# Hybrid S5 / short-conv layer on one core: context tiles normed by ScalarE, first channel block moved forward in the head

## The chip, the cores and the metric

One core of a Trainium2 chip. The metric is the device time of one execution in microseconds (us); less is better. Engines: PE is TensorE, DVE is VectorE, ACT is ScalarE, POOL is GpSimd, SP is SyncE. SP and POOL start DMA transfers, each through a queue of its own (q1 is SP's and ACT's, q0 is POOL's); all transfers share 16 DMA engines.

## What is computed

One layer of a diffusion backbone, cut to what matters here (512 latent tokens, 256 context tokens, 2048 channels):

```python
shift, scale, gate = split(silu(c) @ w_ada + b_ada)      # adaLN, once for c, once for c_ctx
h  = layernorm(x)   * (1 + scale)   + shift              # latent, 512 x 2048
hc = layernorm(ctx) * (1 + scale_c) + shift_c            # context, 256 x 2048
u, z_s5, v, bg, cg, z_cv = split(h @ w_in)
u_c = hc @ w_in[:, :1024]
... state-space scan over u_c then u, GLU, short convolution, output product, gate, layernorm
```

The change is in the layernorms, the adaLN sums and the first products with w_in.

## The kernel before

The kernel writes its instructions in one fixed order; engines run their own instructions in that order and wait for each other by semaphores. The function `head` does everything up to `u` and `u_c`. All products with w_in are in split float32: a weight tile `raw` (128x512, from `w_u`) becomes `whi` (ACT) and `wlo` (DVE, the remainder), a channel block of the input becomes `hi` and `lo`, and three matmuls are added up.

**Token tiles.** Six tiles of 128 tokens x 2048 channels: 0 to 3 latent (x), 4 and 5 context (ctx); x4 and x5 below are the two context tiles. For tile q, `stats(q)` runs four BN_STATS and a BN_AGGR on DVE and a Sqrt on ACT; `norm(q)` makes the reciprocal deviation in five short DVE operations (`rstd_b`) and applies it to the tile in place, one DVE pass over 128x2048 (`wa<-wa,mv,sd`); `turn(q)` transposes the tile on PE in 16 pieces (`acc<-ident,wa`, four to a PSUM bank), and ACT copies each out into the channel-major `xl[k]` (latent) or `xc[k]` (context). DVE takes half of tile 5's copies.

**adaLN.** For each of 16 channel blocks k, `ada(k, 0)` and `ada(k, 1)` multiply one weight tile each (`w_ada`, 1 MB) into `aps`, eight matmuls each. `combine(k)` has two steps: ACT copies `aps` out (`part`); PE transposes it and DVE reduces it into `ss` (shift and scale). `mod(k)` then writes `hi` (ACT) and, in place and `lo`, two DVE operations for each of latent and context. `lat(k)` is nine matmuls of 128x512, `cxt(k, hf)` twelve of 128x256, for each half.

**Buffers and queues.** Token tiles and adaLN tiles share seven 1 MB buffers, `wa` (`RB = 7`). `fill()` gives a new tile the buffer whose last reader stands first in the program. SP's queue takes, in this order: the four latent tiles, w_ada tiles (0,0) and (0,1), x4, three `raw`, x5, then the other `raw` (five buffers of 256 KB). POOL's queue takes all other w_ada tiles, (1,0) and (1,1) first, each as soon as its buffer is free. x5 takes the buffer of tile 0, so SP starts it once tile 0 has been transposed.

**Order.** Tiles 0, 1, 2 are turned, then come `ada(0)`, tile 3, `ada(1)`, `lat(0)`, tile 4, tile 5, `ada(2)`, `cxt(0, 0)`, `mod(1)`, `cxt(0, 1)`, `ada(3)`, `mod(2)`; from there a loop runs one channel block after the other up to k = 15. Behind the head stand some 800 us of products, scan and output, in the same order before and after the change but for the short operations below. A list of planned times (`_Clock`) places background work there.

Of the kernel before, what the change touches and what calls it, by code (L numbers as in the profile page):

```python
# [8 lines left out]
F32 = mybir.dt.float32  # L9
F32R = mybir.dt.float32r  # L10
I32 = mybir.dt.int32
AF = mybir.ActivationFunctionType
OP = mybir.AluOpType

P = 128
# [129 lines left out]
def tile_hybrid_s5_shortconv(  # L145
# [8 lines left out]
    ve, ac = _Timed(nc.vector, "dve", clk), _Timed(nc.scalar, "act", clk)  # L154
# [8 lines left out]
    prm = rest.__enter__()  # L163
# [13 lines left out]
    def slot(name, dt=F32):  # L177
        return base.tile([P, SEQ], dt, name=name, tag="hk", bufs=32)

    def cslot(name, dt=F32):  # L180
        return hcp.tile([P, CTX], dt, name=name, tag="hc", bufs=16)
# [13 lines left out]
    def tt(out, a, b, op, e=None):  # L195
        (e or ve).tensor_tensor(out, a, b, op=op)
# [3 lines left out]
    raws, his = {}, {}  # L200
    items = []

    def pair():
        return [base.tile([P, 512], F32R, name=nm, tag=nm, bufs=3) for nm in ("whi", "wlo")]
# [6 lines left out]
    def load():  # L211
        j = st["load"]
        r = base.tile([P, 512], F32, name="raw", tag="raw", bufs=5)
        sp.dma_start(r, items[j][0])
        raws[j] = r
        st["load"] += 1
# [262 lines left out]
    def head():  # L479
        with pool(name="head", bufs=1) as hp, \  # L480
# [14 lines left out]
            rows, used, near = {}, set(), []  # L495

            def fill(e=None):
                while len(rows) < len(ring):
                    n = len(rows)
                    if n >= RB and ring[n - RB] not in used:  # L500
                        return
                    t = rows[ring[n]] = hp.tile([P, D], F32, name="wa", tag="wa", bufs=RB)
                    a, b = ring[n]
                    if a != "x":
                        (e or gp).dma_start(t, wada_ss[a, b])
                    elif b == 0:
                        for f in range(4):
                            sp.dma_start(t[:, f * 512:(f + 1) * 512], x_in[0:P, f * 512:(f + 1) * 512])
                    else:
                        sp.dma_start(t, x_in[b * P:(b + 1) * P] if b < 4 else ctx_in[(b - 4) * P:(b - 3) * P])  # L510
# [13 lines left out]
            aps, cps = aps[:, 0:256], aps[:, 256:512]  # L524
            for k in range(KT):
                xl[k], xc[k] = slot("xl") if k < KT - 1 else hp.tile([P, SEQ], F32, name="xl15"), cslot("xc")
            sts, rss = {}, {}

            def stats(q):
                stt = hp.tile([P, 4, 6], F32, name="bst", tag="bst", bufs=2)  # L530
                mv = hp.tile([P, 2], F32, name="mv", tag="mv", bufs=2)
                for f in range(4):
                    ve.bn_stats(stt[:, f], rows["x", q][:, f * 512:(f + 1) * 512])
                    yield
                ve.bn_aggr(mv, stt)
                sts[q] = mv
                rss[q] = rstd_a(prm, mv[:, 1:2])
                yield

            def norm(q):  # L540
                yield from rstd_b(rss[q], sts[q][:, 1:2])
                t = rows["x", q]
                ve.tensor_scalar(t, t, sts[q][:, 0:1], rss[q][:, 3:4], op0=OP.subtract, op1=OP.mult)

            def run(*gs):
                gs = list(gs)
                while gs:
                    for g in list(gs):
                        try:
                            next(g)  # L550
                        except StopIteration:
                            gs.remove(g)

            def turn(q):
                t = rows["x", q]
                for k4 in range(4):
                    b = acc[(4 * q + k4) % 7 if q < 4 else 3 + k4]
                    for k in range(4):
                        kk = k4 * 4 + k
                        pe.transpose(b[:, k * P:(k + 1) * P], t[:, kk * P:(kk + 1) * P], ident)  # L560
                    for k in range(4):
                        kk = k4 * 4 + k
                        dst = xl[kk][:, q * P:(q + 1) * P] if q < 4 else xc[kk][:, (q - 4) * P:(q - 3) * P]
                        if q == 5 and k4 > 1:
                            ve.tensor_copy(dst, b[:, k * P:(k + 1) * P])
                        else:
                            ac.activation(dst, b[:, k * P:(k + 1) * P], AF.Copy)
                    if q == 5 and k4 == 0:
                        mod_c(0)
                used.add(("x", q))  # L570
                fill()

            def ada(k, hf):
                w = rows[k, hf].rearrange("p (k c) -> p k c", k=8)
                for j in range(8):
                    pe.matmul(aps[32 * (j % 4):32 * (j % 4) + 32], cs[:, hf * 8 + j], w[:, j],
                              start=hf == 0 and j < 4, stop=hf == 1 and j > 3)
                used.add((k, hf))
                fill()

            def lat(k, whi, wlo):
                lh, ll = hhi[k], hlo[k]
                for m in range(3):
                    wh, wl = whi[:, m * P:(m + 1) * P], wlo[:, m * P:(m + 1) * P]
                    for n_, (w, a) in enumerate(((wh, lh), (wh, ll), (wl, lh))):
                        pe.matmul(acc[m], w, a, start=k == 0 and n_ == 0, stop=k == KT - 1 and n_ == 2)
# [24 lines left out]
            def mod(k, parts, between=None):  # L611
                for x, hi, lo, new, m in parts:
                    hi[k], lo[k] = new("hi", F32R), new("lo", F32R)
                    ac.activation(hi[k], x[k], AF.Identity, scale=ss[:, k, 1, m:m + 1], bias=ss[:, k, 0, m:m + 1])
                if between:
                    between()
                for x, hi, lo, new, m in parts:
                    ve.tensor_scalar(x[k], x[k], ss[:, k, 1, m:m + 1], ss[:, k, 0, m:m + 1], op0=OP.mult, op1=OP.add)
                    tt(lo[k], x[k], hi[k].bitcast(F32), OP.subtract)

            lpart, cpart = (xl, hhi, hlo, slot, 0), (xc, chi, clo, cnear, 1)
# [4 lines left out]
            def mod_c(k):  # L626
                mod(k, [cpart])

            def split(n):
                while st["split"] < n:  # L630
                    j = st["split"]
                    hi, lo = pair()
                    r = raws.pop(j)
                    ac.activation(hi, r, AF.Copy)
                    tt(lo, r, hi.bitcast(F32), OP.subtract)
                    his[j] = (hi, lo)
                    st["split"] += 1
                    if st["load"] < st["split"] + 5:
                        load()

            comb = {k: combine(k) for k in range(KT)}
            run(stats(0))
            run(norm(0))
            run(stats(1))
            turn(0)
            run(norm(1), stats(2))
            turn(1)
            run(norm(2), stats(3))
            turn(2)
            ada(0, 0)  # L650
            ada(0, 1)
            next(comb[0])
            run(norm(3), stats(4))
            split(1)
            turn(3)
            run(stats(5))
            next(comb[0])
            ada(1, 0)
            ada(1, 1)
            n4 = norm(4)  # L660
            mod(0, [lpart], lambda: [next(n4) for _ in range(5)])
            lat(0, *his[0])
            run(n4)
            next(comb[1])
            split(2)
            turn(4)
            run(norm(5))
            next(comb[1])
            turn(5)
            ada(2, 0)  # L670
            ada(2, 1)
            cxt(0, 0, *his.pop(0))
# [56 lines left out]
    def rstd_a(pool, var):  # L729
        sd = pool.tile([P, 4], F32, name="sd", tag="sd", bufs=3)  # L730
        ac.activation(sd[:, 0:1], var, AF.Sqrt, bias=epst)
        return sd

    def rstd_b(sd, var):
        ve.reciprocal(sd[:, 1:2], sd[:, 0:1])
        yield
        ve.tensor_scalar(sd[:, 2:3], var, EPS, sd[:, 1:2], op0=OP.add, op1=OP.mult)
        yield
        tt(sd[:, 2:3], sd[:, 2:3], sd[:, 1:2], OP.mult)
        yield  # L740
        ve.tensor_scalar(sd[:, 2:3], sd[:, 2:3], -0.5, 1.5, op0=OP.mult, op1=OP.add)
        yield
        tt(sd[:, 3:4], sd[:, 2:3], sd[:, 1:2], OP.mult)
        yield

    def put_u(m, lat, cx, t):
# [152 lines left out]
    for k in range(13, KT):  # L899
        keep_item(k)  # L900

    head()


# [574 lines left out]
```

## Time and profile before

| | us |
|---|---|
| median of 3 runs (lowest, highest) | 952.87 (951.29, 953.03) |
| the profiled execution: time | 948.24 |
| its span, first to last instruction | 946.0 |
| TensorE busy in the span | 910.0 (96%) |
| TensorE idle up to 60 us, waiting for normed tiles | 16.5 |

The span is what the trace's views count from; the time lies 2.24 us above it. A view "in order of time" has one row for each run of like instructions; the brackets name what ended the idle time before it. "Stretches" give the busy time of each engine in a window.

### The profile page before, as it was taken

To read this page: it belongs to the slowest core of one execution; us is meant where nothing else is said; L and a number is where in the kernel's file an instruction comes from. 1 tells how busy PE (TensorE), PEld (TensorE's weight loads), DVE (VectorE), ACT (ScalarE), POOL (GpSimd) and SP (SyncE) were. 2 spreads that over 40 slices of the span, in tenths; PEclk is the share of its full clock that TensorE was granted. 3 is DMA by queue.
4 is the path that set the end of the run, shared out by engine and by line. 5 is a ranking of instruction groups with operands and counts; after the bars stand their busy time and mean duration, and the time that the engine had idled before them with its cause. 6 is when DMAs were issued, how large, how long until landed. Compare 5 with 4: busy or idle time off the path is not lost.

```text
span 946.0 us, 15395 instructions
## 1 busy us (share of the span) xinstructions
PE 910.0 (96%) x5488; PEld 745.1 (79%) x5488; DVE 673.1 (71%) x1553; ACT 379.7 (40%) x673; POOL 130.3 (14%) x267
## 2 busy tenths in 40 slices
PE   3899999999999999999999999999999999999994
PEld 3678878788888888888888888888888888886883
DVE  7889883587688889898767384642247879777677
ACT  4643343343343422224446344554444432223322
POOL 2211403120020000001222203020100023310000
PEclk9999999999999999999999999999999999999998
DMA  9999838986394333234566537373586698877322
GB/s 350 423 423 420 346 121 248 341 273 228 126 306 141 97 94 110 92 112 134 145 157 174 158 116 217 105 186 110 153 282 223 210 299 290 283 273 222 124 79 99
DMA packets 97533, 196.08 MB, mean 207 GB/s; under 512 B 26849, under 2 KB 33057, under 8 KB 92721
## 3 DMA queue, kind: packets, MB, share of 16 engines
q1 hardware_dynamic: 67648, 109.10, 35.7%
q0 software_dynamic: 18160, 78.80, 23.3%
q10 hardware_dynamic: 11648, 7.21, 2.4%
q8 instruction: 43, 0.70, 0.3%
q14 instruction: 34, 0.27, 0.1%
HBM read 177.37 MB, written 17.69 MB: 206 GB/s over the span
## 4 chain that ended last, share of the span: by engine, by line
PE 91%; DVE 5%; issue 1%; DMA 1%; ACT 1%; SPq 0%; POOL 0%; DVEq 0%; ACTq 0%; POOLq 0%
PE mm L139 64%; PE bg L139 15%; PE acc L139 9%; PE aps L139 3%; DVE res L139 1%; DVE gacc L139 1%; DMA wa<-in_wada_ss_dram 1%; DVE bst L139 1%; DMA wa<-in_x_dram 1%; DVE owl L139 0%; DVE ept L139 0%; ACT xc L139 0%; DVE wa L139 0%; DVE xc L139 0%; DVE sd L139 0%
## 5 line engine op out<-in xcount | busy, mean ns | idle before, releaser
L139 PE MATMUL mm<-hi,whi 128*128 128x512 f32 x720 | 283.8, 394 | 0.0
L139 PE MATMUL mm<-lo,whi 128*128 128x512 f32 x720 | 280.6, 390 | 0.0
L139 PE MATMUL mm<-hi,wlo 128*128 128x512 f32 x720 | 280.6, 390 | 0.0
L139 DVE TENSOR_TENSOR wlo<-raw,whi 128x512 fp32r<-128x512 f32 x212 | 144.4, 690 | 117.0 <-ACT whi L139 106.9
L139 ACT ACTIVATE whi<-raw 128x512 fp32r<-128x512 f32 x212 | 132.1, 630 | 228.1 <-PE mm L139 157.2
L139 PEld LDWEIGHTS mm<-hi,whi 128*128 128x128 f32 x720 | 135.1, 188 | 31.3 <-issue 2.4
L139 PEld LDWEIGHTS mm<-hi,wlo 128*128 128x128 f32 x720 | 135.2, 188 | 29.4 <-DVE wlo L139 1.0
L139 PEld LDWEIGHTS mm<-lo,whi 128*128 128x128 f32 x720 | 135.3, 188 | 27.1
L139 ACT ACTIVATE owh<-raw 128x512 fp32r<-128x512 f32 x67 | 41.5, 629 | 86.7 <-PE mm L139 36.0
L139 PE MATMUL acc<-hi,whi 128*128 128x256 f32 (+1 forms) x176 | 57.9, 329 | 0.0
L139 DVE TENSOR_TENSOR owl<-raw,owh 128x512 fp32r<-128x512 f32 x67 | 45.7, 686 | 16.8 <-ACT owh L139 16.8
L139 POOL DMA_DIRECT2D gw<-in_wada_g_dram x64 | 34.3, 537 | 156.3 <-DVE gacc L139 124.5
L139 PE MATMUL acc<-lo,whi 128*128 128x256 f32 (+1 forms) x176 | 55.2, 313 | 0.0
L139 PE MATMUL acc<-hi,wlo 128*128 128x256 f32 (+1 forms) x176 | 54.9, 312 | 0.0
L139 DVE SCALAR_TENSOR_TENSOR gacc<-gw,cs,gacc 128x512 f32<-128x512 f32 x60 | 45.0, 750 | 1.3
L139 PEld LDWEIGHTS acc<-hi,whi 128*128 128x128 f32 x176 | 33.2, 189 | 8.4 <-issue 6.2
L139 ACT ACTIVATE hxx<-vst 64x512 f32<-64x512 f32 x32 | 36.1, 1127 | 2.6 <-DVE ks L139 2.3
L139 PEld LDWEIGHTS acc<-hi,wlo 128*128 128x128 f32 x176 | 33.4, 190 | 2.2
L139 PEld LDWEIGHTS acc<-lo,whi 128*128 128x128 f32 x176 | 33.4, 190 | 2.0
L139 PE MATMUL aps<-wa,cs 128*32 128x256 f32 x512 | 31.2, 382 | 3.0 <-DVE ss L139 2.1
L139 DVE TENSOR_TENSOR sc<-MT,vst 128x128 f32<-128x128 f32 x128 | 31.2, 286 | 0.0
L139 PE MATMUL acc<-ident,wa 128*128 128x128 f32 x96 | 15.2, 324 | 16.5 <-DVE wa L139 16.5
(218 smaller groups left out, 1547.0 us busy)
## 6 DMA issues: line engine op xcount, KB each, us to landing
raw<-in_w_m_dram SPq DMA_DIRECT2D x180, 256.0 KB, 2.9
wa<-in_wada_ss_dram POOLq DMA_DIRECT2D x30, 1024.0 KB, 12.3
gw<-in_wada_g_dram POOLq DMA_DIRECT2D x64, 256.0 KB, 5.6
raw<-in_w_out_dram SPq DMA_DIRECT2D x64, 256.0 KB, 4.3
raw<-in_w_u_dram SPq DMA_DIRECT2D x32, 256.0 KB, 8.4
btt<-in_bt_dram POOLq DMA_DIRECT2D x16, 512.0 KB, 6.6
pwt<-Wd POOLq DMA_DIRECT2D x16, 512.0 KB, 5.5
uu<-Ud POOLq DMA_DIRECT2D x16, 384.0 KB, 6.0
```

Source lines behind the costliest of these rows:

```text
L139: return f(*a, **k)
```

## The change

It does five things. (1) The two context tiles are normed by ACT (`norm_a`, one Identity activation with scale and bias over 128x2048) where DVE did it; DVE computes the bias, minus mean by deviation, in one more short operation (`nb`). (2) `rstd_b` has four short operations where it had five; it also serves the four closing layernorms. (3) The first of tile 2's BN_STATS goes ahead of tile 1's norm, which then runs without pieces of `stats(2)` in between. (4) `ada(0)` goes ahead of tile 2 and the second step of `combine(0)` ahead of tile 3; the short operations of tile 4 and `mod(0)` go into tile 3's turn, behind its first four pieces; `stats(5)` follows them; `lat(0)` stands between `ada(1, 0)` and `ada(1, 1)`. (5) `mod_c(0)` stays where it was, passed as an argument.

```diff
--- before.py
+++ after.py
@@ -524,7 +524,7 @@
             aps, cps = aps[:, 0:256], aps[:, 256:512]
             for k in range(KT):
                 xl[k], xc[k] = slot("xl") if k < KT - 1 else hp.tile([P, SEQ], F32, name="xl15"), cslot("xc")
-            sts, rss = {}, {}
+            sts, rss, nbs = {}, {}, {}
 
             def stats(q):
                 stt = hp.tile([P, 4, 6], F32, name="bst", tag="bst", bufs=2)
@@ -540,7 +540,16 @@
             def norm(q):
                 yield from rstd_b(rss[q], sts[q][:, 1:2])
                 t = rows["x", q]
-                ve.tensor_scalar(t, t, sts[q][:, 0:1], rss[q][:, 3:4], op0=OP.subtract, op1=OP.mult)
+                if q < 4:
+                    ve.tensor_scalar(t, t, sts[q][:, 0:1], rss[q][:, 3:4], op0=OP.subtract, op1=OP.mult)
+                    return
+                nb = prm.tile([P, 4], F32, name="sd", tag="sd", bufs=3)[:, 0:1]
+                ve.scalar_tensor_tensor(nb, sts[q][:, 0:1], -1.0, rss[q][:, 3:4], op0=OP.mult, op1=OP.mult)
+                nbs[q] = nb
+
+            def norm_a(q):
+                t = rows["x", q]
+                ac.activation(t, t, AF.Identity, scale=rss[q][:, 3:4], bias=nbs[q])
 
             def run(*gs):
                 gs = list(gs)
@@ -551,7 +560,7 @@
                         except StopIteration:
                             gs.remove(g)
 
-            def turn(q):
+            def turn(q, between=None):
                 t = rows["x", q]
                 for k4 in range(4):
                     b = acc[(4 * q + k4) % 7 if q < 4 else 3 + k4]
@@ -565,8 +574,8 @@
                             ve.tensor_copy(dst, b[:, k * P:(k + 1) * P])
                         else:
                             ac.activation(dst, b[:, k * P:(k + 1) * P], AF.Copy)
-                    if q == 5 and k4 == 0:
-                        mod_c(0)
+                    if between and k4 == 0:
+                        between()
                 used.add(("x", q))
                 fill()
 
@@ -643,30 +652,38 @@
             run(norm(0))
             run(stats(1))
             turn(0)
-            run(norm(1), stats(2))
+            g = stats(2)
+            next(g)
+            run(norm(1))
+            run(g)
             turn(1)
             run(norm(2), stats(3))
-            turn(2)
             ada(0, 0)
             ada(0, 1)
             next(comb[0])
+            turn(2)
             run(norm(3), stats(4))
             split(1)
-            turn(3)
+            next(comb[0])
+            n4 = norm(4)
+
+            def first():
+                run(n4)
+                mod(0, [lpart])
+
+            turn(3, first)
+            norm_a(4)
             run(stats(5))
-            next(comb[0])
             ada(1, 0)
+            lat(0, *his[0])
             ada(1, 1)
-            n4 = norm(4)
-            mod(0, [lpart], lambda: [next(n4) for _ in range(5)])
-            lat(0, *his[0])
-            run(n4)
             next(comb[1])
             split(2)
+            run(norm(5))
             turn(4)
-            run(norm(5))
+            norm_a(5)
             next(comb[1])
-            turn(5)
+            turn(5, lambda: mod_c(0))
             ada(2, 0)
             ada(2, 1)
             cxt(0, 0, *his.pop(0))
@@ -736,11 +753,9 @@
         yield
         ve.tensor_scalar(sd[:, 2:3], var, EPS, sd[:, 1:2], op0=OP.add, op1=OP.mult)
         yield
-        tt(sd[:, 2:3], sd[:, 2:3], sd[:, 1:2], OP.mult)
+        ve.tensor_scalar(sd[:, 2:3], sd[:, 2:3], sd[:, 1:2], -0.5, op0=OP.mult, op1=OP.mult)
         yield
-        ve.tensor_scalar(sd[:, 2:3], sd[:, 2:3], -0.5, 1.5, op0=OP.mult, op1=OP.add)
-        yield
-        tt(sd[:, 3:4], sd[:, 2:3], sd[:, 1:2], OP.mult)
+        ve.tensor_scalar(sd[:, 3:4], sd[:, 2:3], 1.5, sd[:, 1:2], op0=OP.add, op1=OP.mult)
         yield
 
     def put_u(m, lat, cx, t):
```

Three places in the engines' order follow. POOL first, the first six w_ada tiles that wait for a buffer, with what each waits for (`PE_49`: PE's count; `DMAHW0_49`, `DMAHW1_49`: landings of w_ada (0,0) and (0,1); `DMASW...`: landings of POOL's own; `DVE_49`: DVE's). Before:

```order
L139 DMA wa<-in_wada_ss_dram 128x2048 [waits DVE_49,PE_49] x2
L139 DMA wa<-in_wada_ss_dram 128x2048 [waits DMAHW0_49,DMASW0_49,PE_49]
L139 DMA wa<-in_wada_ss_dram 128x2048 [waits DMAHW1_49,DMASW1_49,PE_49]
L139 DMA wa<-in_wada_ss_dram 128x2048 [waits DMASW2_49,DVE_49,PE_49]
L139 DMA wa<-in_wada_ss_dram 128x2048 [waits DMASW6_49,DMASW3_49,PE_49]
```

After:

```order
L139 DMA wa<-in_wada_ss_dram 128x2048 [waits DVE_49,PE_49]
L139 DMA wa<-in_wada_ss_dram 128x2048 [waits DMAHW0_49,PE_49]
L139 DMA wa<-in_wada_ss_dram 128x2048 [waits DMAHW1_49,DMASW0_49,PE_49]
L139 DMA wa<-in_wada_ss_dram 128x2048 [waits DMASW1_49,DVE_49,PE_49]
L139 DMA wa<-in_wada_ss_dram 128x2048 [waits DMASW2_49,DVE_49,PE_49]
L139 DMA wa<-in_wada_ss_dram 128x2048 [waits DMASW6_49,DMASW3_49,PE_49]
```

Before, tiles (1,0) and (1,1) take the buffers of token tiles 1 and 2, and (2,0) and (2,1) those of w_ada (0,0) and (0,1). Now (1,1) and (2,0) take those of (0,0) and (0,1), which are read right behind token tile 1, and only then come the buffers of token tiles 2 and 3.

ACT, from tile 5's Sqrt (`sd`) to the first context `hi`; the `xc` copies of tile 4 are the first four such rows (four copies each, banks 180 to 183), tile 5's begin at the second row on bank 180. Before:

```order
L139 ACTIVATE sd<-mv,epst 128x1
L139 ACTIVATE hi<-xl,ss 128x512
L139 ACTIVATE part<-aps 128x256
L139 ACTIVATE whi<-raw 128x512
L139 ACTIVATE xc<-acc_180 128x128 x4
L139 ACTIVATE xc<-acc_181 128x128 x4
L139 ACTIVATE xc<-acc_182 128x128 x4
L139 ACTIVATE xc<-acc_183 128x128 x4
L139 ACTIVATE xc<-acc_180 128x128 x4
L139 ACTIVATE hi<-xc,ss 128x256
```

After, from tile 4's norm (the first `wa<-wa,sd`) on:

```order
L139 ACTIVATE wa<-wa,sd 128x2048
L139 ACTIVATE sd<-mv,epst 128x1
L139 ACTIVATE part<-aps 128x256
L139 ACTIVATE whi<-raw 128x512
L139 ACTIVATE xc<-acc_180 128x128 x4
L139 ACTIVATE xc<-acc_181 128x128 x4
L139 ACTIVATE xc<-acc_182 128x128 x4
L139 ACTIVATE xc<-acc_183 128x128 x4
L139 ACTIVATE wa<-wa,sd 128x2048
L139 ACTIVATE xc<-acc_180 128x128 x4
L139 ACTIVATE hi<-xc,ss 128x256
```

`hi<-xl,ss` moved up, out of this piece; the two norms moved in, tile 4's ahead of tile 5's Sqrt, tile 5's behind all sixteen copies of tile 4.

DVE, from behind tile 3's norm, before:

```order
L139 TENSOR_TENSOR wlo<-raw,whi 128x512
L139 BN_STATS bst<-wa 128x6 x4
L139 BN_AGGR mv<-bst 128x2
L139 TENSOR_REDUCE ss<-aps 128x4
L139 TENSOR_TENSOR ss<-ss,bss 128x4
L139 TENSOR_SCALAR ss<-ss 128x2
```

(then the short operations of tile 4, `mod(0)` and both norms), and after, from the same place:

```order
L139 BN_AGGR mv<-bst 128x2
L139 TENSOR_TENSOR wlo<-raw,whi 128x512
L139 TENSOR_REDUCE ss<-aps 128x4
L139 TENSOR_TENSOR ss<-ss,bss 128x4
L139 TENSOR_SCALAR ss<-ss 128x2
L139 RECIPROCAL sd<-sd 128x1
L139 TENSOR_SCALAR sd<-mv,sd 128x1
L139 TENSOR_SCALAR sd<-sd 128x1 x2
L139 SCALAR_TENSOR_TENSOR sd<-mv,sd 128x1
L139 TENSOR_SCALAR xl<-xl,ss 128x512
L139 TENSOR_TENSOR lo<-xl,hi 128x512
L139 BN_STATS bst<-wa 128x6 x4
```

Tile 5's BN_STATS stood behind the first `wlo`, ahead of the sums `ss`; they now stand behind `lo<-xl,hi`, the last operation of `mod(0)`.

## Rows read from the trace of the kernel before

**Rows 1.** The page, part 1: busy time, share, instructions.

```profile
PE 910.0 (96%) x5488; PEld 745.1 (79%) x5488; DVE 673.1 (71%) x1553; ACT 379.7 (40%) x673; POOL 130.3 (14%) x267
```

**Rows 2.** PE in order of time: start, length, instructions, [idle before <- releaser].

```profile
11.21 3.67 PE L139 MATMUL acc<-ident,wa 128*128 128x128 f32 x16 [11.21 <-DVE wa L139]
...
18.53 3.63 PE L139 MATMUL acc<-ident,wa 128*128 128x128 f32 x16 [3.64 <-DVE wa L139]
...
34.22 0.50 PE L139 MATMUL acc<-hi,whi 128*128 128x512 f32 x1
...
36.41 1.91 PE L139 MATMUL acc<-ident,wa 128*128 128x128 f32 x16
...
38.42 2.16 PE L139 MATMUL acc<-ident,wa 128*128 128x128 f32 x16
...
40.51 1.93 PE L139 MATMUL aps<-wa,cs 128*32 128x256 f32 x32
...
46.35 1.93 PE L139 MATMUL aps<-wa,cs 128*32 128x256 f32 x32 [0.63 <-DVE ss L139]
```

**Rows 3.** What PE waited for between 0 and 60 us: total, times, longest.

```profile
PE acc L139 <- DVE wa L139: 16.5, 4, 11.2
```

**Rows 4.** Stretches: busy time by engine, granted clock, DMA share, GB/s.

```profile
17.80:21.20 3.40, 2.67 (x13) 2.67 (x14) 3.40 (x11) 1.45 (x8) 0.00 (x0) 0.61 1.01 429
...
53.60:139.00 85.40, 85.40 (x794) 67.88 (x794) 75.78 (x263) 33.33 (x60) 16.14 (x33) 1.00 0.81 326
```

**Rows 5.** DVE in order of time, first 40 us.

```profile
8.78 0.17 DVE L139 RECIPROCAL sd<-sd 128x1 f32<-128x1 f32 x1 [0.36 <-ACT sd L139]
...
9.81 1.35 DVE L139 TENSOR_SCALAR wa<-wa,mv,sd 128x2048 f32<-128x2048 f32 x1
...
11.07 2.47 DVE L139 BATCH_NORM_STATS2 bst<-wa 128x6 f32<-128x512 f32 x4
...
30.90 0.26 DVE L139 BATCH_NORM_AGGREGATE mv<-bst 128x2 f32<-128x24 f32 x1
...
33.44 0.69 DVE L139 TENSOR_TENSOR lo<-xl,hi 128x512 fp32r<-128x512 f32 x1
```

**Rows 6.** ACT in order of time, first 45 us.

```profile
13.87 0.29 ACT L139 ACTIVATE sd<-mv,epst 128x1 f32<-128x1 f32 x1 [5.12 <-DVE mv L139]
...
34.36 0.38 ACT L139 ACTIVATE part<-aps 128x256 f32<-128x256 f32 x1 [1.59 <-PE aps L139]
...
37.05 3.50 ACT L139 ACTIVATE xc<-acc 128x128 f32<-128x128 f32 x20 [1.78 <-PE acc L139]
...
42.79 0.62 ACT L139 ACTIVATE whi<-raw 128x512 fp32r<-128x512 f32 x1
...
43.31 0.80 ACT L139 ACTIVATE hi<-xl,ss 128x512 fp32r<-128x512 f32 x1
...
44.02 0.59 ACT L139 ACTIVATE hi<-xc,ss 128x256 fp32r<-128x256 f32 x1
```

**Rows 7.** POOL in order of time: first transfer that waits for a buffer.

```profile
22.46 0.53 POOL L139 DMA_DIRECT2D wa<-in_wada_ss_dram  x1 [17.15 <-PE acc L139]
```

**Rows 8.** DMA queues 22.5 to 26 us: packets, MB, share of 16 engines.

```profile
q1 hardware_dynamic: 424, 1.50, 104.8%
```

**Rows 9.** DMA queues 27 to 33 us.

```profile
q0 software_dynamic: 282, 2.05, 81.0%
q1 hardware_dynamic: 268, 0.48, 20.9%
```

**Rows 10.** DMA packets by size, 22.2 to 24.6 us.

```profile
DMA packets 400, 1.04 MB, mean 434 GB/s; under 512 B 45, under 2 KB 45, under 8 KB 349
```

**Rows 11.** Transfers issued at 10.54 and 14.92 us: KB, us to landing.

```profile
raw<-in_w_u_dram SPq DMA_DIRECT2D x1, 256.0 KB, 13.9
...
wa<-in_ctx_dram SPq DMA_DIRECT2D x1, 1024.0 KB, 12.6
```

**Rows 12.** DVE in the last 10 us, one of the short operations.

```profile
936.48 0.16 DVE L139 TENSOR_TENSOR sd<-sd 128x1 f32<-128x1 f32 x1
```

## Prediction

> **What bounds the kernel now.** I read the page's busy times first: TensorE is busy 910.0 of 946.0 us [rows 1], so about 36 us can be saved at all. Then where PE is idle: its waits up to 60 us give one line, 16.5 us in four waits for a normed tile (`wa`), the longest 11.2 [rows 3]. PE in order of time shows them at the token tiles: 11.21 us before tile 0, 3.64 before tile 1 [rows 2]. Then the stretches: from 53.60 to 139.00 PE is busy 85.40 of 85.40 us at clock 1.00 while the DMA engines are at 0.81 [rows 4]. So from the block loop on, PE alone sets the time, and the instructions there are those of before. The change can therefore be read at one point: the start of `ada(2)`, 40.51 us [rows 2], the first work behind both context tiles. What that start moves, the end moves, as long as the order behind it has no idle time to swallow a delay. `ada(3)` begins 5.84 us later after a wait of 0.63 for `ss` [rows 2]; that is all the slack I see near it.
>
> Second thing to read: the queues. From 22.5 to 26 us the hardware queue q1 (SP's) is alone and moves 1.50 MB, 0.428 MB/us [rows 8]. POOL's first w_ada transfer that waits for a buffer is issued at 22.46, as soon as tile 1 has been transposed (18.53 + 3.63) [rows 2, 7], and no q0 byte is seen until 26.0: 3.5 us from issue to bytes. From 27 to 33 both queues run: q0 282 packets and 2.05 MB, q1 268 packets and 0.48 MB [rows 9]. The queues get about equal numbers of packets, not of bytes. The `raw` tiles come in rows of 2 KB, w_ada and the context in rows of 8 KB, so a raw beside w_ada gets 0.08 MB/us.
>
> **The change part by part.**
>
> *Tile 1 earlier.* Five short operations and gaps take 9.81 - 8.78 = 1.03 us [rows 5]; four take 0.84, so every norm is 0.19 cheaper. Tile 0 is transposed from 11.0. Tile 1's norm loses the three pieces of `stats(2)` that stood in it: 11.07 - 0.19 + 2.47 (BN_STATS) + 0.26 (aggregate) + 0.7 (one BN_STATS, which covers the Sqrt of 0.29 [rows 6]) + 0.84 + 1.35 (pass) ends at about 16.5 [rows 5], 2.0 us earlier than 18.5. The pieces are paid back in tile 2's norm, so tiles 2 and 3 come out about when they did. By itself this saves nothing behind tile 3.
>
> *POOL's transfer earlier.* This is what I take to decide. It waits for tile 1's transposes alone. These end at 18.5 if they take 1.9 us (tile 4's took 1.91), at 20.1 if they take 3.63 again [rows 2]. I take the first, since PE's idle time before them halves from 3.64 to 1.8. The transfer goes out at 18.7, its bytes begin at 22.2; at the other bound, 23.9. The next three have their buffers behind `ada(0, 0)`, `ada(0, 1)` and tile 2, about 20, 21.5 and 25, so q0 has 4.2 MB to move without a pause. SP's queue still has part of its raws to move then, and x5 stands behind them: in 22.2 to 24.6 there are 349 - 45 = 304 packets of 2 KB, 0.62 MB [rows 10]; before, the third raw (issued 10.54, landing after 13.9) was in at 24.4, x5 (14.92 + 12.6) at 27.5 [rows 11]. Now 0.62 MB at 0.08 MB/us take 7.8 us, to 30.0. Then x5, 8 KB rows against 8 KB rows, gets half of 0.425: 1.05 MB take 4.9 us. **x5 lands at about 35.0 instead of 27.5.** With POOL's bytes from 23.9 the raws would be in alone, and x5 would land at about 29; a POOL stream that takes more than its share, at 36.5. These are the bounds. By 35.0 q0 has moved 0.34 x 7.8 + 0.21 x 4.9 = 3.7 of its 4.2 MB, so it does not run dry.
>
> *A rule that says otherwise.* The Trainium skill ("DMA: Bandwidth & Descriptors", section "SWDGE vs HWDGE vs iDMA") calls 4096 B the preferred upper size of a packet and the DMA engine's context-switching boundary. By that rule two rows of a raw would go per turn, x5 would land near 31.5, and the time would be that of rival A. The packet counts, 268 against 282 [rows 9], speak for single rows.
>
> *Statistics of tile 5 moved back, its norm to ACT.* Before, tile 5's BN_STATS ended at 30.9 (the aggregate starts at 30.90), ahead of `ss`; `lo` ended at 33.44 + 0.69 = 34.13 [rows 5]. Now `stats(5)` stands behind `lo`, which goes 2.5 us forward on DVE but must wait for tile 3's first copies and `hi` (0.80) on ACT [rows 6]: I put its end at 32.2. What follows is a chain, and each link is an instruction of a row: last of BN_STATS 2.47 after the landing (they can't start before it), aggregate 0.26 [rows 5], Sqrt 0.29, then ACT in its program's order: `part` 0.38 and `whi` 0.62, which overlap a little, 0.8 together; sixteen `xc` copies of tile 4 (3.50 / 20 = 0.175 each) 2.80; then the norm [rows 6]. Queued behind the waiting Sqrt are thus all copies of tile 4, whose work is ready long before; PE waits for the norm behind them. DVE's five short operations of tile 5 lie beside the copies and cost nothing as long as these take over 1.0 us. The ACT pass over 128x2048 is in no row. From `hi` at 512 and 256 columns (0.80 and 0.59 [rows 6]) each 256 columns cost 0.21 to 0.22, so 2048 cost 0.80 + 6 x 0.22 = 2.1. Bounds: DVE's 1.35 [rows 5] and four passes of 0.80, 3.2. Sum behind the landing: 2.47 + 0.26 + 0.29 + 0.8 + 2.80 + 2.1 = 8.7. **Tile 5's transposes start at 35.0 + 8.7 = 43.7 instead of 38.42** [rows 2]: +5.3.
>
> The Trainium skill ("ScalarE: Activation LUTs", "Rules for kernel authors") wants multiply and add on VectorE, up to about 3 times as fast per element in bf16. As an estimate from that page three times 1.35 is 4.05 us for each norm, and the sum would be 1.9 higher. The slope of rows 6 gives 1.6 times, and the data are float32; no row shows the pass itself.
>
> *The clock.* Tile 4, `lat(0)` and `ada(1)` keep their order before tile 5. `lat(0)` takes 2.2 us (34.22 to 36.41 [rows 2]) from 32.2, so with `ada(1, 1)` and tile 4 PE is done at about 37 and then idle for some 6.5 us. Before, an idle time of 3.64 us was followed by 16 transposes of 3.63 us [rows 2] in a stretch with a granted clock of 0.61 [rows 4], about the lower of the two levels (1.2 and 2.4 GHz) for most of it. So tile 5 takes 3.63 instead of 2.16 [rows 2]: +1.5 (bounds 0 and 1.7).
>
> *The rest.* `lat(0)`'s products, `ada(0)` and the sums `ss` of block 0 are moved forward into time in which PE or DVE waits anyway; with tile 5 late that saves nothing at `ada(2)`. Tile 4's norm on ACT (2.1 us) lies behind tile 3's copies and ahead of the Sqrt, before x5 lands, so its cover is the landing; without it, it stands in the chain above with up to 2 us. The closing layernorms run the short operations on DVE behind each other; the one that stands at the end saves 0.16 plus a gap, 0.2 [rows 12]. The other three lie beside PE.
>
> **Sum:** +5.3 + 1.5 - 0.2 = +6.6. The profiled execution (948.24: span 946.0 plus 2.24) would become 954.8. The median of the runs is 952.87, 4.6 above the profiled one; the change is the same in both: **959.5 us**.
>
> **Rivals.**
>
> *A: the landing does not bind.* x5 lands before 32.2 if the queues take turns so that two rows of 2 KB go against one of 8 (a third of 0.425, 0.14 MB/us; the raws end at 26.6, x5 at 31.5), or if POOL's bytes begin at 23.9. Then the order on ACT alone counts: 32.2 + 8.7 = 40.9, +2.5, the clock 0 to 1.5, less 0.2: 955.2 to 956.7. For it: the bounds above. Against: the equal packet counts [rows 9].
>
> *B, the other side: not slower.* PE would go on without a wait: `lat(0)` to 34.4, `ada(1, 1)`, tile 4 to 37.3, tile 5 to 39.4, and `ada(2)` 1.1 us earlier than before; with the tail 951.6, with a `lo` 0.6 earlier 951.0. This takes a norm of tile 5 finished by 37.3, so x5 landed by 28.6 and its statistics ahead of `lo`. The order of DVE and ACT excludes the second, unless DVE and ACT finish `mod(0)` by 28.6, 5.5 us sooner than before. It decides from there.
>
> *C: no difference that shows.* The delay reaches `ada(2)` and is swallowed later: PE's idle time behind it would have to shrink by 5 us or more, and it has 0.63 there and none from 53.6 to 139 [rows 2, 4]. About 952.9.
>
> **How the numbers follow.** The forecast's own mechanism, from 956.7 (x5 landing at 32.5) to 962.5 (landing at 36.5, norm of 3.2), 0.70; A 0.14; B 0.06; C 0.06; worse than 962.5, by a clock that stays low beyond tile 5, 0.04. The range 955.0 to 962.5 takes in the forecast and A, 0.84 less their edges, about 0.8. About 0.2%, 1.9 us, is what a measurement of this kernel can tell from no change; only the best of B and a gain that I do not see get past that: faster 0.05, same 0.08, slower 0.87.
>
> **What the profile after would show.** Right: tile 1's transposes at about 16.5; POOL's first waiting transfer at 18.7; a third raw that lands near 30 and x5 near 35; ACT's norm of 2.1 us at about 41.5, with copies of tile 4 held behind the Sqrt; PE idle some 6 us before tile 5, released by ACT `wa`; `ada(2)` at 47 or later; PE's busy time much as before. Wrong: x5 in before 32 (then A), an ACT pass near 1.3 us or beyond 3.2, BN_STATS of tile 5 without a wait for DMA, transposes of tile 5 at 2 us in spite of the idle time, or an idle time behind 55 us that was not there.

## The result and the profile after

The changed kernel takes 957.34 us (median of 22 runs, 951.37 to 961.61) against 951.48 for the kernel before (22 runs). The ratio is 1.0057, interval 1.0047 to 1.0068: slower by 5.4 us (5.9 between the medians), where 6.6 were forecast. The profiled execution took 951.37 us, span 949.1; it is the fastest of the 22, so it shows less than the usual delay. I took two more traces of the same kernel (below as second and third): 958.2 and 954.05 us. The three differ, and the account rests on their differences.

The first trace. The page's busy times: PE works as long as before [rows 1], so the time is waiting.

```profile
PE 909.7 (96%) x5488; PEld 744.7 (78%) x5488; DVE 670.7 (71%) x1543; ACT 383.1 (40%) x675; POOL 129.4 (14%) x267
```

PE in order of time, the rows that answer to [rows 2]:

```profile
10.84 3.67 PE L139 MATMUL acc<-ident,wa 128*128 128x128 f32 x16 [10.84 <-DVE wa L139]
16.26 3.32 PE L139 MATMUL acc<-ident,wa 128*128 128x128 f32 x16 [1.75 <-DVE wa L139]
...
35.38 1.97 PE L139 MATMUL acc<-ident,wa 128*128 128x128 f32 x16
...
41.13 1.97 PE L139 MATMUL acc<-ident,wa 128*128 128x128 f32 x16 [3.56 <-ACT wa L139]
43.03 1.93 PE L139 MATMUL aps<-wa,cs 128*32 128x256 f32 x32
...
48.86 1.93 PE L139 MATMUL aps<-wa,cs 128*32 128x256 f32 x32 [0.62 <-DVE ss L139]
```

Tile 4 is done at 37.4, a microsecond sooner than before. Then PE waits 3.56 us for a tile that ACT norms, a releaser that did not exist before, and `ada(2)` starts at 43.03 instead of 40.51 [rows 2]: +2.5. The span is 3.1 us longer. What ACT and DVE did in that time (the same view of these engines):

```profile
34.74 0.29 ACT L139 ACTIVATE sd<-mv,epst 128x1 f32<-128x1 f32 x1
...
36.32 2.81 ACT L139 ACTIVATE xc<-acc 128x128 f32<-128x128 f32 x16
38.84 2.24 ACT L139 ACTIVATE wa<-wa,sd 128x2048 f32<-128x2048 f32 x1
```

```profile
31.34 0.69 DVE L139 TENSOR_TENSOR lo<-xl,hi 128x512 fp32r<-128x512 f32 x1
31.95 2.46 DVE L139 BATCH_NORM_STATS2 bst<-wa 128x6 f32<-128x512 f32 x4
```

The statistics begin right behind `lo`, without a wait for a transfer. POOL's first waiting transfer and the landings of the third raw and of x5 (in order of time; then the transfers, KB and us to landing):

```profile
19.87 0.54 POOL L139 DMA_DIRECT2D wa<-in_wada_ss_dram  x1 [14.55 <-PE acc L139]
```

```profile
raw<-in_w_u_dram SPq DMA_DIRECT2D x1, 256.0 KB, 15.1
...
wa<-in_ctx_dram SPq DMA_DIRECT2D x1, 1024.0 KB, 15.9
```

The raw, issued at 10.32, is in at 25.4; x5, issued at 14.54, at 30.4, 2.9 later than before [rows 11] and still 1.5 ahead of its statistics. In this execution rival A is the whole story. The second trace is another matter. Its PE, DVE, ACT, POOL and transfers:

```profile
16.68 1.97 PE L139 MATMUL acc<-ident,wa 128*128 128x128 f32 x16 [1.74 <-DVE wa L139]
...
45.48 3.64 PE L139 MATMUL acc<-ident,wa 128*128 128x128 f32 x16 [4.73 <-ACT wa L139]
49.05 1.93 PE L139 MATMUL aps<-wa,cs 128*32 128x256 f32 x32
```

```profile
36.89 2.47 DVE L139 BATCH_NORM_STATS2 bst<-wa 128x6 f32<-128x512 f32 x4 [4.39 <-DMA wa<-in_ctx_dram]
```

```profile
39.69 0.29 ACT L139 ACTIVATE sd<-mv,epst 128x1 f32<-128x1 f32 x1 [4.52 <-DVE mv L139]
```

```profile
18.95 0.54 POOL L139 DMA_DIRECT2D wa<-in_wada_ss_dram  x1 [13.64 <-DVE mv L139]
```

```profile
raw<-in_w_u_dram SPq DMA_DIRECT2D x1, 256.0 KB, 19.8
...
wa<-in_ctx_dram SPq DMA_DIRECT2D x1, 1024.0 KB, 21.9
```

Tile 1's transposes take 1.97 us and POOL goes out at 18.95. The third raw (issued 10.65) lands at 30.5, x5 (14.97) at 36.9, DVE waits 4.39 us for it, and ACT's queue stands behind the Sqrt for 4.52. This is the forecast's chain link by link: 18.7, 30.0 and 35.0 were written down, though x5 came 0.4 us behind the upper bound of 36.5. PE has little to do from 37.8 on, then turns tile 5 in 3.64 us. The stretch around it (span, PE and other busy times, granted clock 0.52, DMA):

```profile
45.40:49.10 3.70, 3.62 (x20) 3.33 (x24) 1.14 (x4) 1.95 (x10) 0.00 (x0) 0.52 0.79 328
```

That is the lower of the two levels (1.2 and 2.4 GHz), and `ada(2)` starts 8.5 us later than before.

### The profile page after: what moved, and what is told of

It is laid out like the page before. It is cut to its first block, busy times and chain, and to the rows that moved or that the text cites. A ratio compares the mean times of both kernels' runs of the same rounds, so it can differ in the third digit from the quotient of the medians.

```text
span 949.1 us, 15386 instructions
## 1 busy us (share of the span) xinstructions
PE 909.7 (96%) x5488; PEld 744.7 (78%) x5488; DVE 670.7 (71%) x1543; ACT 383.1 (40%) x675; POOL 129.4 (14%) x267
## 4 chain that ended last, share of the span: by engine, by line
PE 88%; DVE 5%; DMA 3%; ACT 2%; issue 1%; SPq 0%; ACTq 0%; DVEq 0%
PE mm L139 62%; PE bg L139 14%; PE acc L139 8%; PE aps L139 3%; DMA Ud<-ut 2%; DVE bst L139 1%; DVE res L139 1%; DVE gacc L139 1%; DMA gate<-in_b_g_dram 1%; DMA wa<-in_x_dram 0%; DVE wa L139 0%; DVE owl L139 0%; DVE sd L139 0%; ACT xc L139 0%; DVE ept L139 0%
## 5 line engine op out<-in xcount | busy, mean ns | idle before, releaser
L139 PEld LDWEIGHTS mm<-lo,whi 128*128 128x128 f32 x720 | 135.2, 188 | 27.1
```

Source lines behind the costliest of these rows:

```text
L139: return f(*a, **k)
```

## The experiments

All kernels compute the whole reference. In each, the order behind the head is that of the changed kernel.

**The changed kernel again, twice.** No edit.

> The changed kernel once more, for its trace: the profiled execution had a mean clock of 0.996 and was the fastest of 22, most others show 0.988 and 2 to 10 us more. Theory 'clock': the order of events up to tile 5 is the same (tile 5 from about 41), and a stretch at half clock lies behind PE's idle time in the head, some 10 to 15 us long, which costs the rest. Theory 'late landing': x5 lands at 33 or later in this execution and PE's wait before tile 5 is longer than 3.6 us at full clock.

Measured: a part of each theory, in one execution. x5 landed at 36.9, and the transposes behind the wait ran at the low clock, in a stretch of some 7 us (42 to 49) and not of 10 to 15.

> The changed kernel a third time, for its trace. In the first, tile 1's transposes took 3.32 us, POOL's transfer went out at 19.87 and x5 landed at 30.41; in the second 1.97, 18.95 and 36.87. If the moment of that transfer against the rest of the raws decides, x5 lands at 34 or later here where tile 1 takes about 2 us and POOL goes at 18.7 to 19.1, and before 32 where tile 1 takes 3.3 us or more; time 955 to 959 in the first case, 951 to 955 in the second.

Measured: tile 1 in 2.71 us, POOL at 19.96, x5 (17.0 us from 15.01) in at 32.0, 954.05 us. Tile 1's time lies between the two cases foreseen; the landing and the time are at the edge of the second. Tile 5:

```profile
41.86 3.63 PE L139 MATMUL acc<-ident,wa 128*128 128x128 f32 x16 [3.56 <-ACT wa L139]
45.42 1.93 PE L139 MATMUL aps<-wa,cs 128*32 128x256 f32 x32
```

The wait is that of the first trace, 3.56 us, but the transposes take 3.63 instead of 1.97. So the two extra costs come apart: late landing in one trace of three, the low clock behind the wait in two of three. With `ada(2)` 2.5, 8.5 and 4.9 us later than before, the three times are 3.1, 10.0 and 5.8 above before's profiled 948.24.

**The shorter `rstd_b` alone.**

```diff
-        tt(sd[:, 2:3], sd[:, 2:3], sd[:, 1:2], OP.mult)
-        yield
-        ve.tensor_scalar(sd[:, 2:3], sd[:, 2:3], -0.5, 1.5, op0=OP.mult, op1=OP.add)
+        ve.tensor_scalar(sd[:, 2:3], sd[:, 2:3], sd[:, 1:2], -0.5, op0=OP.mult, op1=OP.mult)
         yield
-        tt(sd[:, 3:4], sd[:, 2:3], sd[:, 1:2], OP.mult)
+        ve.tensor_scalar(sd[:, 3:4], sd[:, 2:3], 1.5, sd[:, 1:2], op0=OP.add, op1=OP.mult)
```

(and `mod(0)` takes in four of tile 4's short operations where it took five)

> The kernel before with the four-operation rstd_b alone. The forecast's term: 0.2 us less in the tail, tiles normed a little earlier, ratio 0.9998. Rival: a side effect of the interleaving, one yield fewer puts the pass of a norm ahead of the next tile's aggregate, so its Sqrt is no longer covered and tiles 2 to 4 come up to 0.5 us later each; PE then reaches ada(2) 0 to 0.7 us later, ratio 1.000 to 1.001.

Measured: ratio 1.0015 (0.9993 to 1.0036), `ada(2)` at 41.42, 0.9 us later than before [rows 2] where the rival allowed 0.7. No gain shows, and the rival is not settled by this.

**ACT norms alone**, in the order of before, with `nb` and `norm_a` as in the change.

```diff
             run(n4)
+            norm_a(4)
...
             run(norm(5))
+            norm_a(5)
```

> The kernel before, its order and its five-operation rstd_b kept, with tiles 4 and 5 normed by ACT where DVE stood. Theory 'ACT order': tile 5's pass stands behind sixteen copies of tile 4, tile 5's transposes start at 41 to 41.5 and ada(2) at 43 to 43.5 (before 40.51), as in the changed kernel, with x5 landing at 27.5 as before; ratio 1.003 to 1.006. Theory 'late landing' (the forecast): without POOL's earlier transfer only the slower pass counts, 0.9 us or so; ada(2) at about 41.4, ratio 1.001.

Measured: 955.8 us, ratio 1.0063 (1.0042 to 1.0085). Nothing else of the change is in this kernel, and its loss is as large as that of the whole change. In its trace x5 landed at 27.2, as before, and `ada(2)` started at 46.06, later than either theory said. Some 2.2 us of that came ahead of tile 4, from a later `lat(0)` that ran at a granted clock of 0.51, and the rest from the wait before tile 5. PE in order of time:

```profile
38.60 2.00 PE L139 MATMUL acc<-ident,wa 128*128 128x128 f32 x16
...
44.16 1.97 PE L139 MATMUL acc<-ident,wa 128*128 128x128 f32 x16 [3.34 <-ACT wa L139]
```

**Tile 5 back on DVE**, all else as changed.

```diff
-                if q < 4:
+                if q != 4:
...
-            split(2)
             run(norm(5))
+            split(2)
             turn(4)
-            norm_a(5)
```

> The changed kernel with tile 5 normed by DVE, right behind its short operations and ahead of the second wlo; tile 4 stays on ACT, the order of all else too. Theory 'ACT order': tile 5 is normed at about 37.4, PE goes on without a long wait, ada(2) at 39.3 to 39.6 (changed kernel 43.03, before 40.51); ratio to before 0.998 to 0.9995. Theory 'late landing': x5 lands late in most executions, statistics wait for it and ada(2) comes at 42 or later; ratio 1.002 or more.

Measured: 950.38 us, ratio 1.0006 (0.9990 to 1.0021): the loss is gone, but nothing is gained. Its trace is that of the second slowest of 12 executions (954.69 us): x5 landed at 35.2, so this one paid the other cost (DVE in order of time):

```profile
35.23 2.47 DVE L139 BATCH_NORM_STATS2 bst<-wa 128x6 f32<-128x512 f32 x4 [2.44 <-DMA wa<-in_ctx_dram]
```

**Two raws behind x5 in SP's queue**, in the changed kernel.

```diff
             fill(sp)
-            for _ in range(3):
-                load()
+            load()
...
             turn(0)
+            load()
+            load()
```

> The changed kernel with one line of SP's queue moved: the second and third raw are asked for behind x5 instead of ahead of it. x5 has 8 KB rows, so beside w_ada it gets half and lands at 25.5 to 28 in every execution. Theory 'late landing and ACT order together': the statistics then start at 32 behind lo, tile 5's transposes at 41 (the changed kernel: 41.1 in one trace, 45.5 in the other), ada(2) at 43; median 953.5 to 955.5, ratio to before 1.002 to 1.0045. Theory 'ACT order alone': the landing costs nothing, so nothing changes, median 957, ratio 1.0055 to 1.007.

Measured: 954.99 us, ratio 1.0043 (1.0028 to 1.0058). POOL went out at 18.82, as early as in the second trace, but x5 landed at 29.6 (25.5 to 28 was foreseen), ahead of its statistics at 32.25, and tile 5 started at 41.45. The intervals of 1.0043 and 1.0057 overlap: the landing costs about 1.3 us by the ratios and 2.5 by the medians, not sharply told from nothing.

**The same with tile 5 on DVE** (both edits).

> The same with tile 5 normed by DVE ahead of the second wlo (the run before with DVE had x5 landing at 35.2 and a median level with before). Theory 'late landing and ACT order together': both costs gone, ada(2) at 39.3 to 39.7, 1 us earlier than before's 40.51; median 948.5 to 950, ratio 0.997 to 0.999. Theory 'ACT order alone': no gain over the run with DVE and late raws, ratio 1.000 to 1.001.

Measured: 949.43 us, ratio 0.9978 (0.9969 to 0.9988). Against the kernel with tile 5 on DVE and the raws ahead of x5 (1.0006) that is 2.7 us for the queue's order alone (1.7 by the medians), and the intervals do not overlap. Its trace is that of the slowest of 12 executions (952.03 us), with tile 0 at 12.29 and `ada(2)` at 41.23, where 39.3 to 39.7 was foreseen; counted from tile 0 this is 0.4 us earlier than before.

**POOL held back.** The changed kernel, `fill()` of tile 1's turn moved behind a copy that waits for tile 3's mean.

```diff
             run(norm(2), stats(3))
+            gp.tensor_copy(hold, sts[3][:, 0:1])
+            fill()
```

> The changed kernel with POOL's first waiting w_ada transfer held back by a one-column copy on POOL that reads tile 3's mean (at about 22.9), so that it goes out about when it did before (22.46). Nothing of SP's queue is changed. Theory 'POOL's earlier transfer makes x5 late': x5 lands at 27.5 to 29, tile 5's transposes at 41 to 41.5, as if the raws stood behind x5; median 953.5 to 956. Rival: x5's landing is late for another reason (SP's own queue, the order of raws), and it lands at 30 or later here too, median 957.

Measured: POOL at 23.79, and x5 at 27.1 with SP's queue untouched:

```profile
23.79 1.58 POOL L139 DMA_DIRECT2D wa<-in_wada_ss_dram  x3
```

```profile
wa<-in_ctx_dram SPq DMA_DIRECT2D x1, 1024.0 KB, 12.0
```

So POOL's earlier transfer is what delays x5. Tile 5 started at 41.67, behind 3.57 us of wait for ACT, and took 3.67; 956.3 us, ratio 1.0053 (1.0034 to 1.0072), between what the two sides foresaw. An early landing alone shows no saving here while the ACT pass stands where it does, but six runs, in which three w_ada tiles go out late as well, can't tell 1.3 us from nothing.

**Statistics first** in the interleaved places.

```diff
-            run(norm(2), stats(3))
+            run(stats(3), norm(2))
```

(and the same for tiles 3 and 4)

> The kernel with raws behind x5 and tile 5 on DVE, and in the two interleaved places the statistics of the next tile put ahead of the norm's operations (statistics first, so that the Sqrt is covered by a BN_STATS and the aggregate stands ahead of the pass again). If the shorter rstd_b made tiles 3 and 4 later by uncovering the Sqrt (0.4 us of wait at each), tile 3 is transposed 0.4 to 0.9 us earlier and ada(2) starts at 38.6 to 39.2; ratio 0.996 to 0.9985. If not, as the run before.

Measured: tile 3 is transposed 0.9 us earlier, counted from tile 0, and `ada(2)` starts at 39.28; 949.26 us, ratio 0.9978 (0.9967 to 0.9988), the same as without. What was won in the head does not show in the time. In this execution some 1.6 us are lost at about 145 us, behind short waits that the kernel before has too, in a stretch with a granted clock of 0.62:

```profile
142.50:147.00 4.50, 4.50 (x19) 3.78 (x18) 0.69 (x1) 0.87 (x2) 3.56 (x4) 0.62 0.51 146
```

The same loss stands in six of the fourteen traces (not in that of before, nor in the three of the changed kernel), so one trace's end can't be set against another's without it.

**PE kept busy before tile 5**, in the changed kernel with raws behind x5.

```diff
             norm_a(5)
+            for _ in range(20):
+                pe.transpose(cps[:, 0:P], ident, ident)
             next(comb[1])
```

> The changed kernel with the raws behind x5, and twenty added transposes of the identity (2.4 us at full clock, their result is thrown away) in PE's idle time before tile 5, ahead of the transposes of the part sums. Theory 'clock': tile 5's transposes still start at 41 to 41.5 from the span's start, but at full clock (1.97 instead of the 2.7 to 3.7 seen in three traces), ada(2) at 43.2 and no half-clock stretch behind it; median 953 to 954, 1 to 2 us under the run without them. Rival 'only the order counts': median as without them, 955, or later by what the added work delays.

Measured: 952.43 us, ratio 1.0015 (1.0004 to 1.0026), 0.28% or 2.7 us under the run without them by the ratios (2.1 by the medians), for added work; the intervals do not overlap. PE in order of time, and the stretch from tile 5 on, granted clock 1.00:

```profile
38.18 2.35 PE L139 MATMUL aps<-ident 128*128 128x128 f32 x20
...
42.12 1.97 PE L139 MATMUL acc<-ident,wa 128*128 128x128 f32 x16 [1.38 <-ACT wa L139]
44.02 1.93 PE L139 MATMUL aps<-wa,cs 128*32 128x256 f32 x32
```

```profile
42.10:46.00 3.90, 3.88 (x49) 2.79 (x50) 1.85 (x8) 1.94 (x9) 1.05 (x2) 1.00 1.01 420
```

Without the twenty transposes the row of tile 5 and `ada(2)` read 2.71 and 2.80 us instead of 1.97 and 1.93:

```profile
41.45 2.71 PE L139 MATMUL acc<-ident,wa 128*128 128x128 f32 x16 [3.56 <-ACT wa L139]
44.09 2.80 PE L139 MATMUL aps<-wa,cs 128*32 128x256 f32 x32
```

Counted from tile 0, `ada(2)` ends 1.6 us earlier with the transposes. That much of the 2.7 the two traces show in the head; the trace without them also has the loss at about 145 us.

**Tile 5's ACT pass ahead of tile 4's copies**, raws behind x5.

```diff
+            run(norm(5))
+            norm_a(5)
             split(2)
-            run(norm(5))
             turn(4)
-            norm_a(5)
```

> The changed kernel with the raws behind x5, and tile 5's ACT pass put ahead of the second whi and the sixteen copies of tile 4, its short operations ahead of the second wlo. Theory 'place behind the copies': the pass runs at 36.1 to 38.3, tile 5's transposes start near 39.5 but wait for tile 4's copies, which now come behind the pass and hold the same banks; ada(2) about 1 us earlier than with the pass behind them, ratio 1.001 to 1.003. Theory 'duration of the pass' (2.2 against 1.35 on DVE): the place costs nothing, no change, ratio 1.0035 to 1.005.

Measured: 953.38 us, ratio 1.0023 (1.0008 to 1.0038), 1.9 us under the pass behind them, with overlapping intervals. The wait changes its releaser, as foreseen, to the copies that hold the banks:

```profile
40.30 2.67 PE L139 MATMUL acc<-ident,wa 128*128 128x128 f32 x16 [1.96 <-ACT xc L139]
```

**No ACT norm at all.** Raws behind x5, statistics first, both context tiles on DVE, tile 4 between `lo` and `stats(5)`; the rest of the change stands.

```diff
             def norm_a(q):
                 t = rows["x", q]
-                ac.activation(t, t, AF.Identity, scale=rss[q][:, 3:4], bias=nbs[q])
+                ve.tensor_scalar(t, t, sts[q][:, 0:1], rss[q][:, 3:4], op0=OP.subtract, op1=OP.mult)
```

> The kernel with raws behind x5, statistics first and tile 5 on DVE, with tile 4 normed by DVE too, between lo and the statistics of tile 5: no ACT norm is left, the rest of the change stands. The pass takes 1.3 us on DVE in the chain to tile 5. If tile 4's ACT norm is the part that gains, ada(2) comes 1 to 1.3 us later than with it, ratio 0.9985 to 1.000; if moving the work forward is what gains, as with it, 0.997 to 0.9985.

Measured: 948.39 us, ratio 0.9970 (0.9959 to 0.9982), the lowest median of all, faster than both kernels. PE in order of time:

```profile
37.03 1.94 PE L139 MATMUL acc<-ident,wa 128*128 128x128 f32 x16 [1.17 <-DVE wa L139]
38.89 1.93 PE L139 MATMUL aps<-wa,cs 128*32 128x256 f32 x32
```

So without the ACT norms, what is left of the change is a gain once the raws stand behind x5 and the statistics go first, and tile 4's norm on ACT adds nothing that shows. Which part gains, the first channel block moved forward or another, is not separated: no run has the new order of SP's queue on the kernel before.

## Why the prediction came out

The direction, the place (`ada(2)`) and the time held: 957.3 where 959.5 stood, inside 955.0 to 962.5. Of the 2.2 us between them 1.4 come from the start: 952.87 was the median of three runs, 951.48 that of 22. The weights inside the sum held less well, and that their errors nearly cancel is luck: a landing that binds in one trace of three was priced as if it did in each, and the clock was priced low. Four of the signs of being wrong that the prediction lists did show: x5 in before 32 and tile 5 in 2 us in the first trace, statistics without a wait for DMA in the first and third, and new idle time behind 55 us in all three (see the tail).

- *The chain on ACT.* Right, link by link: 0.29, then `part`, `whi`, sixteen copies in 2.8, then the pass. In the three traces the pass takes 2.19 to 2.24 us where 2.1 was read off the slope of [rows 6]; against DVE's 1.35 [rows 5] that is 1.6 to 1.7 times. The Trainium skill ("ScalarE: Activation LUTs", "Rules for kernel authors") points the right way, towards VectorE, but its 3 times, stated for bf16, is not seen on these float32 rows.
- *The step that held only in part: "This is what I take to decide", POOL's earlier transfer.* The mechanism is real (held back, x5 lands at 27.1; in the second trace 18.95, 30.5 and 36.9), but its size in the sum was taken from one case. I took tile 1's transposes at 1.9 us; they took 3.32, 1.97 and 2.71, POOL went out at 19.87, 18.95 and 19.96, and x5 landed at 30.4, 36.9 and 32.0. Only the second comes after `lo` and binds. From the second trace to the others POOL goes out about 1 us later and x5 lands 4.9 to 6.4 us earlier. That the raws ahead of x5 get a small share as soon as q0 runs fits this, but does not explain each landing (last section). The 2.8 us that the landing had in the sum (35.0 against 32.2) are 1.3 by the ratios and 2.5 by the medians, with overlapping intervals, and 2.7 and 1.7 with tile 5 on DVE: in none of the four readings more than was forecast.
- *The packets.* From 24.5 to 30.4 us of the second trace both queues again had equal numbers of packets, and bytes by their size:

```profile
q0 software_dynamic: 230, 1.67, 67.0%
q1 hardware_dynamic: 233, 0.88, 36.3%
```

  There the Trainium skill's packet of up to 4096 B ("DMA: Bandwidth & Descriptors", "SWDGE vs HWDGE vs iDMA", in a table on the software queue's descriptors) does not show as two raw rows a turn. From the second raw (landed at 27.3) to the third (30.5), 0.26 MB took 3.15 us, the forecast's 0.08 MB/us. From there x5 took 6.4 us and not 4.9. Between 30.5 and 36.9 the packets were equal again, but the bytes far from halves:

```profile
q0 software_dynamic: 257, 1.88, 70.6%
q1 hardware_dynamic: 258, 0.74, 28.6%
```

- *The clock term, +1.5, looks too small.* The place was right, and in the second and third trace the price of tile 5 as well (3.64 and 3.63 against 3.63). With PE kept busy the time falls by 2.7 us by the ratios, 2.1 by the medians; the head of the traces shows 1.6 of it, and the intervals do not exclude 1.5. The 22 runs of the changed kernel fit: each execution with a mean granted clock of 0.989 or less took 957.2 us or more, each one with 0.990 or more 957.1 or less. Where tile 5 only partly ran at the low level, `ada(2)` paid the rest, 2.80 instead of 1.93.
- *Rival A* gave 2.3 to 3.8 us more than before for an x5 that lands in time; the kernel with raws behind x5 measures 4.1 by the ratio, 3.4 by the medians. This is the larger part of the truth. By the ratios the 5.4 us are some 1.4 for ACT's order less what the work moved forward gains (with PE kept busy), 2.7 for the clock behind its wait, and 1.3 for the landing; by the medians 1.3, 2.1 and 2.5. The intervals leave each of the last two open by nearly 2 us either way, so which of them is the larger is not shown.
- *Rival B*, the gain, needed tile 5's statistics ahead of `lo`; the order excluded that. The other way to it is the DVE pass of 1.35 in place of 2.8 of copies and 2.2 of pass: with the raws behind x5 that reaches 0.9978, without any ACT norm 0.9970.
- *The tail.* From the last `ept` to the last `res` DVE needs 0.1 us less, not 0.2. And what `ada(2)` shows is not quite what the end shows: behind the block loop 0.7 to 1.5 us more were lost in the three traces (in the best kernel, of 1.6 us won at `ada(2)`, 0.3 was left at PE's end). Nearly all of it is waiting: 0.6 to 1.0 us between 180 and 190 us, where before has none of that size, and one wait at about 857 us that is 0.2 to 0.6 us longer than before. In the first trace, and last the row of before that answers to the second:

```profile
187.15 0.50 PE L139 MATMUL mm<-hi,whi 128*128 128x512 f32 x1 [0.62 <-ACT whi L139]
...
857.10 0.50 PE L139 MATMUL mm<-owl,OSh 128*128 128x512 f32 x1 [1.54 <-DVE owl L139]
```

```profile
853.87 0.50 PE L139 MATMUL mm<-owl,OSh 128*128 128x512 f32 x1 [1.30 <-DVE owl L139]
```

  So "PE alone sets the time" does not hold all the way to the end; why these waits grow is open.
- *Two bounds of the forecast's range* do not come out of its own terms. An x5 at 32.5 gives 957.0 and not 956.7, and one at 36.5 with a pass of 3.2 gives at most 962.3 and not 962.5. Nothing hangs on it.

## What to carry to other kernels

An operation that moves to an idle engine joins that engine's queue: its price is its own duration plus everything that stands ahead of it there, here sixteen copies for which nobody hurried. A wait on TensorE can cost more than its length: here one of 3.56 us was followed by 1.7 us of lost clock in one trace and by none in another, and filling it with throw-away work gained 2 to 3 us. And an earlier transfer on one queue can be a later one on the other: here, moving the small rows of two raws behind the urgent tile was worth 1.3 to 2.7 us.

## What was not expected of the hardware

The first sixteen transposes take 3.67 us in the first trace, as in before [rows 2], although the granted clock of their stretch reads 1.00:

```profile
11.00:14.90 3.90, 3.51 (x16) 3.11 (x16) 3.73 (x11) 1.41 (x9) 0.00 (x0) 1.00 1.02 431
```

The same work takes 1.94 to 1.97 later on. The next sixteen, 1.7 to 2.0 us behind, take anything from 1.97 to 3.68 in traces of kernels with the same order up to there. The clock column shows this in part: it reads 1.00 beside 3.32 in the first trace, and 0.69 beside 2.71 in the third. POOL's transfer waits for these transposes, so the scatter moves it from one execution to the next. It doesn't explain the landing alone: with tile 5 on DVE POOL went out at 20.04 and x5 landed at 35.2, later than in the third trace with 19.96 and 32.0. What else sets it is open.
